# First products of five and six blocks made ahead at the opening of an FFN

## The chip, the cores and the metric

The kernel runs as one program on one core of a Trainium2 chip. The metric is device microseconds of one execution, from the first to the last instruction and what lies around them; a median over several runs stands for a kernel. One further execution was profiled, and its trace is what the rows below are from. Engines are named as the profile names them: PE is the matmul engine and PEld its weight loads, DVE, ACT and POOL are the vector, scalar and GpSimd engines, SP issues the transfers.

## The reference, cut to what matters

Two layers work on 512 latent tokens and, in the first layer, 256 context tokens of width 1024. Each layer mixes tokens with three groups of heads, projects out, and then runs a SwiGLU FFN of hidden width 2816 between two norms. All data are 32-bit floats.

```python
def swiglu(h, w13, w2):
    gate, up = jnp.split(h @ w13, 2, axis=-1)
    return (jax.nn.silu(gate) * up) @ w2

for l in range(DEPTH):
    ...
    lat = lat + gt1 * rms_norm(mixed_l, norm_mix_post[l])
    h_l = modulate(rms_norm(lat, norm_ffn_pre[l]), sh2, sc2)
    lat = lat + gt2 * rms_norm(swiglu(h_l, ffn_w13[l], ffn_w2[l]), norm_ffn_post[l])
    if not last:
        ...
        cx = cx + cgt2 * rms_norm(swiglu(h_c, ffn_w13[l], ffn_w2[l]), norm_ffn_post[l])
```

The change lies in `h @ w13`, the up-projection, where it begins.

## The kernel before

**Precision.** Every operand of a matmul is split into two parts: `hi`, the value cast to a shorter float format (on ACT, L368 for weights, L1303 for activations), and `lo`, the rest (a subtraction on DVE, L369 and L1304). A product is three matmuls per 128 rows of the inner dimension: hi by hi, hi by lo, lo by hi (`prod`, L1320, matmuls at L1324).

**The up-projection.** The hidden width is cut into 22 blocks of 128 (`NF`). For each block, gate and up are made together by Strassen's scheme in Winograd's form: the inner dimension is halved, the tokens are halved (`hn` is 384 in layer 0 and 256 in layer 1), and gate and up are the two halves of the weights. Seven products replace eight. Each is over 4 inner blocks of 128, so it has 12 matmuls. The activations' side gives `b11`, `b21`, `b22` and the sums `t1` to `t4` (`combine`, L1307); the weights' side gives `a11`, `a12` (the gate's two halves), `a22` and the sums `s1` to `s4`, made per block in `load13` (L399): two on POOL (L417, L418) and two on DVE (L419, L420). `s2` to `s4` lie in a tile `S` with one buffer.

**Loads.** `load13` brings a block's weights into a tile `raw`: block numbers that are odd use the one in pool `F`, even ones the one in pool `wp`. Each of the two has one buffer. A full block is two transfers of 512 KB (`fetch(0)` for up, `fetch(2)` for gate, L405). A gate-only load (`gate_only`) is one transfer of 512 KB. The pieces are then cast and subtracted into `whi` and `wlo`, four buffers each, of 1024 columns.

**Made ahead.** The two products with `b11` and `b21` need only the first half of the tokens, whose norms are finished first. For the first `NA` blocks the kernel loads the gate alone (`u["w13a"]`), makes the product `a11` by `b11` (`up_first`, L1327, its result copied to `uu` at L1329) and later adds `a12` by `b21` (`up_gate`, L1331, SiLU into `g1` at L1333). Between the two the result stays open in a bank of the accumulator memory: pool `psm` has two banks (`mm`), `psx` five (`px`), `psa` one (`pa`). When such a block's turn comes in `ffn_up` (L1335) its weights are loaded again, in full, since the sums need all four quarters, but `a11` and `a12` are not split again (`late`), and five products are left. A block with nothing made ahead runs all seven.

**Order.** `begun` is filled in block order (from L1367), then `b21` is split, then the gate products follow, then `combine`, then `ffn_up` for all 22 blocks. The code's order gives priorities; a scheduler at compile time places each instruction on its engine's queue by them and by when it expects operands and buffers to be there. On the chip each queue runs in that fixed order. `get(i, 0)` loads a unit only when it is asked for; `get(i)` also loads the one after it, so full blocks 0 and 1 are asked for together.

**Space.** `uu` and `g1` have `NA + 1` buffers in pool `FB`, on the right side of the memory; `F` holds `raw`, `S`, `hf`, `u3` and `g2`.

Of the kernel before, what the change touches and what calls it, by code (L numbers as in the profile page):

```python
# [11 lines left out]
F32 = mybir.dt.float32  # L12
# [70 lines left out]
def tile_backbone(ctx: ExitStack, tc: tile.TileContext, a: dict, out: bass.AP, dbg=None):  # L83
# [9 lines left out]
    psa = ctx.enter_context(tc.tile_pool(name="psa", bufs=1, space=PSUM))  # L93

    def mm():
        return psm.tile([128, 512], F32, tag="mm", name="mm")

    def px():
        return psx.tile([128, 512], F32, tag="px", name="px")

    def pt(pool, tag, shape, dt=F32, bufs=None):
        kw = {} if bufs is None else {"bufs": bufs}
        return pool.tile(shape, dt, tag=tag, name=tag, **kw)
# [164 lines left out]
    def kblk(src):  # L268
        return src.rearrange("(k p) n -> p k n", p=128)
# [84 lines left out]
    def add(name, shape, srcs, prem=None, hook=None):  # L354
        specs.append((name, shape, srcs, prem, hook))
        return len(specs) - 1
# [75 lines left out]
    def get(i, ahead=1):  # L432
        while state["next"] <= min(i + ahead, len(specs) - 1):
            j = state["next"]
            if specs[j][0] == "wo" and j > i:
                break
            load(j)
            state["next"] += 1
        return state["units"].pop(i)
# [3 lines left out]
    def w_unit(name, src, c0, n, prem=None):  # L443
        return add(name, [128, 8, n], [((allsl,), kblk(src[:, c0:c0 + n]))], prem)
# [3 lines left out]
    for l in range(NL):  # L448
        wi = a["w_in"][l]
        u = U[l]  # L450
        if l > 0:
            u["gv"] = w_unit("gv", wi, 256, 256)
        u["small"] = add("small", [128, 8, 80],
                         [((allsl, allsl, slice(0, 32)), kblk(wi[:, 768:800])),
                          ((allsl, allsl, slice(64, 80)), kblk(wi[:, 2336:2352]))],
                         hook=lambda raw: G.memset(raw[:, :, 32:64], 0.0))
        u["xbc"] = {j: w_unit("xbc", wi, 1312 + 256 * j, 256) for j in (2, 3, 0, 1)}
        u["gqk"] = w_unit("gqk", wi, 0, 256)
        u["rk"] = w_unit("rk", wi, C_RET + 256, 256)
        u["rq"] = w_unit("rq", wi, C_RET, 256)  # L460
        u["rv"] = w_unit("rv", wi, C_RET + 512, 256)
        if l == 0:
            u["gv"] = w_unit("gv", wi, 256, 256)
        u["gr"] = w_unit("gr", wi, 512, 256)
        u["rg"] = w_unit("rg", wi, C_RET + 768, 256)
        for j in range(2):
            u[f"z{j}"] = w_unit("z", wi, 800 + 256 * j, 256)
        u["wo"] = [w_unit("wo", a["w_out"][l], 256 * j, 256, l) for j in range(4)]
        u["w13"], u["w2"] = {}, {}
        w13 = a["ffn_w13"][l]  # L470

        NA = 4
        u["NA"] = NA

        def add13(f, gate_only, late):
            return add("w13", None, {"f": f, "gate_only": gate_only, "late": late,
                                     0: kblk(w13[:, FF + 128 * f:FF + 128 * f + 128]),
                                     2: kblk(w13[:, 128 * f:128 * f + 128])})

        u["w13a"] = [add13(f, True, False) for f in range(NA)]  # L480
        for f in range(NF):
            u["w13"][f] = add13(f, False, f < NA)
        u["passes"] = [(j, range(6 if l + 1 < NL else 4)) for j in range(2)]
        for pi, (j, _) in enumerate(u["passes"]):
            f0 = 0
            for gi, gn in enumerate(GROUPS):
                u["w2"][gi, pi] = add("w2", [128, gn, 512],
                                      [((allsl,), kblk(a["ffn_w2"][l, 128 * f0:128 * (f0 + gn),
                                                                   512 * j:512 * j + 512]))])
                f0 += gn  # L490
# [9 lines left out]
    def gemm_a(unit, csl, m, seg, cut=False):  # L500
        t0, n = seg
        ps = mm()
        w = [(lambda k, t=t: t(k)[:, csl]) for t in unit]
        step = 256 if cut else n
        for o in range(0, n, step):
            h = [(lambda k, t=t: t[:, k, t0 + o:t0 + o + step]) for t in H["t"]]
            gemm3(ps[:m, o:o + step], w, h, 8)
        return ps
# [77 lines left out]
    for l in range(NL):  # L586
# [60 lines left out]
        with ExitStack() as sx:  # L647
# [16 lines left out]
            with pool(f"Sa{l}") as Sa:  # L664
# [14 lines left out]
                for t0, n in segs_all[::-1]:  # L679
                    ps = opened.pop(("small", t0), None) or gemm_a(un, slice(0, 80), 80, (t0, n), True)  # L680
# [7 lines left out]
                for d in range(2):  # L688
                    zz = pt(Sa, f"gz{d}", [128, T])
                    ee = pt(Sa, f"ge{d}", [128, T])  # L690
                    for t0, n in segs_all:
                        ps = px()
# [53 lines left out]
            with scx:  # L746
                for fb in (4, 5, 6, 7, 0, 1, 2, 3):
# [5 lines left out]
                    for t0, n in segs[::-1]:  # L753
# [4 lines left out]
                        ps = gemm_a(un, slice(128 * (fb % 2), 128 * (fb % 2) + 128), 128, (t0, n), fb in (4,))  # L758
# [14 lines left out]
                    if fb < 4:  # L773
                        ps = [px(), px()]
# [99 lines left out]
            for j in range(2):  # L874
                for t0, n in (segs_out if j == 0 else segs_all):
                    ps = gemm_a(un, slice(128 * j, 128 * j + 128), 128, (t0, n))
# [391 lines left out]

        NA = u["NA"]
        hview = hds[l].rearrange("f p t -> p f t")  # L1270
# [14 lines left out]
        with pool(f"F{l}") as F:  # L1285
            state["F"] = F
            def ut(tag, bufs=2):
                return pt(FB if tag in ("uu", "g1") else F, tag, [128, hn], bufs=bufs)

            uus = [ut("uu", NA + 1) for _ in range(NA)]  # L1290
            g1s = [ut("g1", NA + 1) for _ in range(NA)]
            bh = pt(FB, "bh", [128, 2, 4, hn], F32R, bufs=1)
# [27 lines left out]
            def prod(ps, un, wn, rn, first):  # L1320
                w, r = un[wn], rhs[rn]
                for k in range(4):
                    for p, (x, y) in enumerate(((0, 0), (0, 1), (1, 0))):
                        PE.matmul(ps[:, :hn], w[x][:, k], r[y](k), start=first and k == 0 and p == 0,  # L1324
                                  stop=k == 3 and p == 2, skip_group_check=True)

            def up_first(pa, un, uu):  # L1327
                prod(pa, un, "a11", "b11", True)
                S.copy(uu, pa[:, :hn])  # L1329

            def up_gate(pa, un, g1):  # L1331
                prod(pa, un, "a12", "b21", False)
                S.activation(g1, pa[:, :hn], AF.Silu)  # L1333

            def ffn_up(f, begun):  # L1335
                un = get(u["w13"][f])
                hf = pt(F, "hf", [128, tot], bufs=2)
                h1, h2 = hf[:, :hn], hf[:, hn:]
                if begun is None:
                    pa = mm()  # L1340
                    uu, g1 = ut("uu", NA + 1), ut("g1", NA + 1)
                    up_first(pa, un, uu)
                else:
                    uu, g1 = begun
                pb = px()
                prod(pb, un, "s2", "t2", True)
                V.tensor_tensor(uu, uu, pb[:, :hn], ALU.add)
                pc = px()
                prod(pc, un, "s3", "t3", True)
                u3 = ut("u3")  # L1350
                V.tensor_tensor(u3, uu, pc[:, :hn], ALU.add)
                pd = px()
                prod(pd, un, "s1", "t1", True)
                V.tensor_tensor(h2, u3, pd[:, :hn], ALU.add)
                if begun is None:
                    up_gate(pa, un, g1)
                prod(pc, un, "a22", "t4", False)
                V.tensor_tensor(h1, uu, pc[:, :hn], ALU.add)
                G.tensor_tensor(h1, h1, g1, ALU.mult)  # L1359
                prod(pd, un, "s4", "b22", False)  # L1360
                V.tensor_tensor(uu, uu, pd[:, :hn], ALU.add)
                g2 = ut("g2")
                S.activation(g2, uu, AF.Silu)
                G.tensor_tensor(h2, h2, g2, ALU.mult)
                DMA.dma_start(hds[l][f], hf)

            begun = []  # L1367
            for f in range(NA):
                un = get(u["w13a"][f], 0)
                ps = mm() if f < 2 else px()  # L1370
                up_first(ps, un, uus[f])
                begun.append((ps, un))
            for i in range(n2):
# [12 lines left out]
            for f in range(NF):  # L1386
                ffn_up(f, begun.get(f))
                if f == 9:
                    for i in range(2):
                        he = pt(FB, "tm", [128, 2, 2, tot], F32R)  # L1390
                        hr = pt(HR, "hr", [128, 2, tot], bufs=1)
                        hid_load(hr, 2 * i)
                        early[2 * i] = hid_split(hr, he[:, 0], he[:, 1])
# [26 lines left out]
        with pool(f"D{l}") as Dp:  # L1420
# [30 lines left out]
            for pi, (j, poss) in enumerate(u["passes"]):  # L1451
# [3 lines left out]
                f = 0  # L1455
# [45 lines left out]
```

## Time and profile before

| | us |
|---|---|
| runs of the kernel | 1896.44, 1889.72, 1876.48 |
| median | 1889.72 |
| the profiled execution | 1883.05 |
| its span, first to last instruction | 1881.3 |
| PE busy in it | 1744.7 (93%) |
| DVE, ACT, POOL busy | 1169.3, 793.0, 560.7 |
| mean granted PE clock | 0.959 of full speed |

In rows of a timeline the first number is the start in us from the span's start, the second the time until the row's last instruction ends, then engine, line, operation, tile written and tiles read, shapes and a count (x2: two such in a row). What stands in square brackets is how long the engine was idle before the row, and what ended it. The trace writes `u` for `u3`, `g` for `g1` and `g2`, `H` for tiles of that tag whatever their name in the code (`whole`, `ta`, `tb_`), and `cst` and `araw` for the two parts of `b11`.

### The profile page before, as it was taken

Reading aid. Unit: us, or ns where it says so; the run is one execution under the profiler, and the core shown is the slowest. Engines: PE = TensorE matmul, PEld = TensorE weight load, DVE = VectorE, ACT = ScalarE, POOL = GpSimd, SP = SyncE. Lnnn points to the kernel's source line nnn. Section 1 sums busy time; section 2 is a strip of 40 time slices with the busy share of each in tenths; the row PEclk is TensorE's granted clock in tenths of the full one; section 3 lists DMA queues with packets and bytes.
Section 4 is the critical chain, followed back from the end, with each engine's and each line's share of the span. In section 5 each row is a group of like instructions: output and inputs, shape, how many; then the busy total and the mean of one; then the engine's idle time right before and its main releaser. Section 6 shows DMA issues by size and latency. Waiting matters only on the chain. (4 is left out here: it accounts for less than half of the span.)

```text
span 1881.3 us, 30313 instructions
## 1 busy us (share of the span) xinstructions
PE 1744.7 (93%) x11851; PEld 1576.0 (84%) x11851; DVE 1169.3 (62%) x1981; ACT 793.0 (42%) x1433; POOL 560.7 (30%) x569
## 2 busy tenths in 40 slices
PE   4999999999879999999899989999987969999998
PEld 3778887798879999999788777889876969999886
DVE  4586787557557655554334446678766568888455
ACT  3545343225654333333323465444423544444343
POOL 1002622104303432332312240073312226555322
PEclk9999999999989999999999989999977989999999
DMA  8535457415325433332645374345613245444663
GB/s 277 183 103 171 136 188 262 156 46 177 113 68 145 140 105 93 93 93 90 240 140 184 116 235 134 112 147 171 214 53 124 84 129 153 125 138 130 245 209 128
DMA packets 239228, 275.15 MB, mean 146 GB/s; under 512 B 14056, under 2 KB 182476, under 8 KB 239084
## 3 DMA queue, kind: packets, MB, share of 16 engines
q1 hardware_dynamic: 237872, 271.30, 45.0%
q8 instruction: 93, 1.52, 0.3%
q10 hardware_dynamic: 1212, 1.91, 0.3%
q14 instruction: 51, 0.42, 0.1%
HBM read 234.24 MB, written 38.93 MB: 145 GB/s over the span
## 5 line engine op out<-in xcount | busy, mean ns | idle before, releaser
L369 DVE TENSOR_TENSOR wlo<-raw,whi 128x1024 fp32r<-128x1024 f32 (+2 forms) x192 | 264.1, 1382 | 160.0 <-ACT whi L368 159.7
L1324 PE MATMUL px<-H,whi 128*128 128x384 f32 (+1 forms) x1408 | 307.6, 310 | 7.4 <-ACT whi L368 7.3
L368 ACT CAST whi<-raw 128x1024 fp32r<-128x1024 f32 (+2 forms) x192 | 194.0, 1018 | 221.6 <-PE px L1324 86.3
L498 PE MATMUL mm<-whi,H 128*128 128x256 f32 x1376 | 275.5, 295 | 11.3 <-ACT stg L630 5.3
L498 PEld LDWEIGHTS mm<-whi,H 128*128 128x128 f32 x1376 | 224.1, 197 | 26.1 <-issue 12.7
L1324 PEld LDWEIGHTS px<-H,whi 128*128 128x128 f32 x1408 | 235.1, 190 | 10.2 <-ACT whi L368 9.5
L1324 PE MATMUL px<-H,wlo 128*128 128x384 f32 (+1 forms) x704 | 211.5, 310 | 0.9 <-DVE wlo L369 0.8
L498 PE MATMUL mm<-wlo,H 128*128 128x256 f32 x688 | 200.6, 292 | 0.0
L498 PE MATMUL mm<-H,whi 128*128 128x256 f32 (+2 forms) x640 | 160.9, 342 | 6.8 <-ACT xp L759 4.4
L368 ACT CAST whi<-S 128x1024 fp32r<-128x1024 f32 x88 | 73.5, 835 | 165.3 <-DVE S L419 84.6
L498 PEld LDWEIGHTS mm<-wlo,H 128*128 128x128 f32 x688 | 135.4, 197 | 3.1 <-issue 2.1
L1324 PEld LDWEIGHTS px<-H,wlo 128*128 128x128 f32 x704 | 131.6, 190 | 1.7 <-DVE wlo L369 1.7
L498 PEld LDWEIGHTS mm<-H,whi 128*128 128x128 f32 (+1 forms) x640 | 109.5, 190 | 26.0 <-ACT xp L759 6.2
L1278 POOL TENSOR_TENSOR hidlo<-hr,hidhi 128x768 fp32r<-128x768 f32 (+1 forms) x40 | 69.7, 1745 | 191.1 <-ACT hidhi L1277 184.7
L498 PE MATMUL px<-whi,H 128*128 128x256 f32 x640 | 120.5, 288 | 3.9 <-ACT H L1235 2.2
L1359 POOL TENSOR_TENSOR hf<-hf,g 128x384 f32<-128x384 f32 (+1 forms) x44 | 55.2, 1255 | 223.2 <-issue 147.0
L369 DVE TENSOR_TENSOR wlo<-S,whi 128x1024 fp32r<-128x1024 f32 x88 | 89.3, 1015 | 40.6 <-ACT whi L368 40.5
L1407 PE MATMUL px<-wlo,hidhi 128*128 128x512 f32 x276 | 108.7, 394 | 0.0
L498 PE MATMUL mm<-H,wlo 128*128 128x256 f32 (+3 forms) x320 | 108.3, 339 | 0.0
L1407 PE MATMUL px<-whi,hidhi 128*128 128x512 f32 x276 | 107.8, 393 | 0.0
L498 PEld LDWEIGHTS px<-whi,H 128*128 128x128 f32 x640 | 101.3, 193 | 6.3 <-ACT H L1235 3.2
L1407 PE MATMUL px<-whi,hidlo 128*128 128x512 f32 x276 | 106.1, 389 | 0.0
(334 smaller groups left out, 4086.0 us busy)
## 6 DMA issues: line engine op xcount, KB each, us to landing
raw<-ffn_w_dram SPq DMA_DIRECT2D x100, 512.0 KB
araw<-ada_w_dram SPq DMA_DIRECT2D x96, 512.0 KB
raw<-w_in_dram SPq DMA_DIRECT2D x26, 1024.0 KB
raw<-ffn_w_dram SPq DMA_DIRECT2D x20, 1024.0 KB
hr<-hd SPq DMA_DIRECT2D x22, 768.0 KB
hr<-hd SPq DMA_DIRECT2D x22, 512.0 KB
Rt<-gd SPq DMA_DIRECT2D x40, 256.0 KB
hd<-hf SPq DMA_DIRECT2D x22, 384.0 KB
```

The source lines that it names most:

```text
L368: S.copy(hi, src)
L369: lo_engine.tensor_tensor(lo, src, hi.bitcast(F32), ALU.subtract)
L498: PE.matmul(ps, x(k), y(k), start=(k == 0 and p == 0), stop=(k == total - 1 and p == 2))
L1278: (G if q else V).tensor_tensor(lo[:, q], hr[:, q], hi[:, q].bitcast(F32), ALU.subtract)
L1324: PE.matmul(ps[:, :hn], w[x][:, k], r[y](k), start=first and k == 0 and p == 0, stop=k == 3 and p == 2, skip_group_check=True)
L1359: G.tensor_tensor(h1, h1, g1, ALU.mult)
L1407: PE.matmul(ps, lh[x](k), rh[y](k), start=f + k == 0 and p == 0, stop=f + k == NF - 1 and p == 2, skip_group_check=True)
```

## The change

The number of blocks made ahead is 5 in layer 0 and 6 in layer 1, in place of 4 in both. `u3` has one buffer in place of two. Block 2's product is kept open in the `pa` bank in place of a `px` bank; blocks 0 and 1 stay in `mm`, and blocks from 3 on are in `px`.

```diff
-        NA = 4
+        NA = 5 if l == 0 else 6
         u["NA"] = NA
...
                 prod(pc, un, "s3", "t3", True)
-                u3 = ut("u3")
+                u3 = ut("u3", 1)
                 V.tensor_tensor(u3, uu, pc[:, :hn], ALU.add)
...
             for f in range(NA):
                 un = get(u["w13a"][f], 0)
-                ps = mm() if f < 2 else px()
+                ps = mm() if f < 2 else px() if f > 2 else psa.tile([128, 512], F32, tag="pa", name="pa")
                 up_first(ps, un, uus[f])
                 begun.append((ps, un))
```

`NA` also sets which full blocks are `late`, the number of gate-only units, and the buffers of `uu` and `g1`. There is one gate-only transfer of 512 KB more in layer 0 and two in layer 1.

## Rows read from the trace of the kernel before

**Rows 1.** The page: busy time and share of the span by engine.

```profile
PE 1744.7 (93%) x11851; PEld 1576.0 (84%) x11851; DVE 1169.3 (62%) x1981; ACT 793.0 (42%) x1433; POOL 560.7 (30%) x569
```

**Rows 2.** Busy time by stretch: both openings, and layer 0's steady part between them.

```profile
core 0: us, PE busy (x) PEld busy (x) DVE busy (x) ACT busy (x) POOL busy (x), PEclk, DMA share, GB/s
543.30:576.55 33.25, 19.55 (x96) 17.80 (x94) 25.13 (x43) 21.52 (x38) 3.65 (x4) 0.79 0.39 111
660.00:700.00 40.00, 40.00 (x232) 40.00 (x231) 24.70 (x32) 15.09 (x21) 10.17 (x10) 1.00 0.25 74
1501.10:1533.43 32.33, 18.19 (x115) 16.07 (x113) 22.40 (x37) 18.71 (x35) 5.24 (x4) 0.79 0.40 114
```

**Rows 3.** PE's waits, layer 0's opening: us in total, times, longest.

```profile
PE px L306 <- ACT xn L297: 4.9, 1, 4.9
PE px L1324 <- ACT whi L368: 3.2, 1, 3.2
```

**Rows 4.** PE's waits, layer 1's opening.

```profile
PE px L1324 <- ACT whi L368: 2.5, 2, 2.3
```

**Rows 5.** POOL's timeline: the first sum of a full block, both layers.

```profile
572.06 1.29 POOL L417 TENSOR_TENSOR S<-raw 128x512 f32<-128x512 f32 x1 [22.74 <-DMA raw<-ffn_w_dram]
...
602.50 1.29 POOL L417 TENSOR_TENSOR S<-raw 128x512 f32<-128x512 f32 x1
...
612.90 1.30 POOL L417 TENSOR_TENSOR S<-raw 128x512 f32<-128x512 f32 x1
...
671.70 1.29 POOL L417 TENSOR_TENSOR S<-raw 128x512 f32<-128x512 f32 x1
...
861.48 1.29 POOL L417 TENSOR_TENSOR S<-raw 128x512 f32<-128x512 f32 x1
...
1528.93 1.28 POOL L417 TENSOR_TENSOR S<-raw 128x512 f32<-128x512 f32 x1 [17.30 <-DMA raw<-ffn_w_dram]
...
1554.94 1.29 POOL L417 TENSOR_TENSOR S<-raw 128x512 f32<-128x512 f32 x1 [0.63 <-DVE wlo L369]
...
1563.23 2.27 POOL L417 TENSOR_TENSOR S<-raw 128x512 f32<-128x512 f32 x1
...
1616.06 1.29 POOL L417 TENSOR_TENSOR S<-raw 128x512 f32<-128x512 f32 x1
...
1735.10 1.29 POOL L417 TENSOR_TENSOR S<-raw 128x512 f32<-128x512 f32 x1
```

**Rows 6.** SP's timeline: requests for weights, layer 0 (block 2, 3, full 0, full 1).

```profile
535.27 0.38 SPq L405 DMA_DIRECT2D raw<-ffn_w_dram  x1
...
563.20 0.38 SPq L405 DMA_DIRECT2D raw<-ffn_w_dram  x1
...
564.34 0.99 SPq L405 DMA_DIRECT2D raw<-ffn_w_dram  x2
...
569.68 0.99 SPq L405 DMA_DIRECT2D raw<-ffn_w_dram  x2
```

**Rows 7.** SP's waits, layer 0's opening: us in total, times, longest.

```profile
SPq L405 <- DVE wlo L369: 14.1, 3, 11.0
```

**Rows 8.** SP's timeline: requests for weights, layer 1 (block 3, full 0, full 1).

```profile
1520.42 0.38 SPq L405 DMA_DIRECT2D raw<-ffn_w_dram  x1
...
1521.56 1.01 SPq L405 DMA_DIRECT2D raw<-ffn_w_dram  x2
...
1527.13 0.99 SPq L405 DMA_DIRECT2D raw<-ffn_w_dram  x2
```

**Rows 9.** ACT's timeline: casts of gate-only weights and block 0's SiLU.

```profile
556.69 1.99 ACT L368 CAST whi<-raw 128x1024 fp32r<-128x1024 f32 x2
...
561.95 0.49 ACT L1333 ACTIVATE g<-mm 128x384 f32<-128x384 f32 x1 [0.57 <-PE mm L1324]
...
567.29 1.05 ACT L368 CAST whi<-raw 128x1024 fp32r<-128x1024 f32 x1 [1.55 <-DMA raw<-ffn_w_dram]
...
1524.79 1.05 ACT L368 CAST whi<-raw 128x1024 fp32r<-128x1024 f32 x1 [1.43 <-DMA raw<-ffn_w_dram]
```

**Rows 10.** DVE's timeline, layer 1: the subtraction of block 3's gate weights.

```profile
1525.87 1.22 DVE L369 TENSOR_TENSOR wlo<-raw,whi 128x1024 fp32r<-128x1024 f32 x1 [0.87 <-ACT whi L368]
```

## The prediction

> **What bounds the kernel now.** I read the page first. TensorE (PE) is busy for 1744.7 us of the 1881.3 us span [rows 1], so the kernel is bound by matmuls and can gain only where PE waits, about 137 us spread over the whole span. Next came the table of stretches, for the places that the change touches. In the stretch that opens layer 0's FFN PE works 19.55 us of 33.25, in layer 1's 18.19 of 32.33, both at a mean granted clock of 0.79; in the middle of layer 0's up-projection it works 40.00 of 40.00 [rows 2]. So the two openings hold some 28 us of idle PE, and the rest of the up-projection none worth naming in layer 0. The change can pay only in these two openings.
>
> The third view is who PE waited for there. The longest wait is for the last token block's normalised rows (4.9 us in layer 0) and the last one before the first full block is for a `whi` cast: 3.2 us in layer 0 [rows 3], 2.5 us in layer 1 [rows 4]. That last wait ends the opening, so I followed it backwards. The cast needs the sums made on POOL, and POOL's first L417 starts at 572.06 only when its data lands, after 22.74 us of idleness [rows 5]. The data was asked for at 564.34 [rows 6], and that request stood waiting on SyncE's queue (SP) for a `wlo` subtraction on VectorE (DVE): 14.1 us in three waits [rows 7]. The `wlo` frees the landing tile `raw`. There are two `raw` tiles, one for even blocks and one for odd, each with a single buffer. **The opening is bound by the turns of these two tiles**, not by a lack of products that PE could make: load, cast on ScalarE (ACT), subtract on DVE, next load. Layer 1 shows the same: requests at 1520.42, 1521.56 and 1527.13 [rows 8], POOL starting at 1528.93 after 17.30 us idle, on the DMA [rows 5].
>
> **The change, part by part.**
>
> *A fifth gate-only load in layer 0, a fifth and a sixth in layer 1.* Block 4's gate load goes through the even tile after block 2's and ahead of full block 0; block 5's goes through the odd tile ahead of full block 1. So full block 0's request moves back by one turn of the even tile. The landing is priced with the gate load of block 3: requested at 563.20 [rows 6], its cast started at 567.29, ended by the DMA [rows 9], so 4.09 us; in layer 1 1520.42 to 1524.79, 4.37 us [rows 8, 9]. The new load is requested 1.14 us behind that one and shares the queue: 4.09 + 1.14 = 5.2 us. Add the cast of 1.05 us [rows 9] and the subtraction of 1.22 us [rows 10]: 5.2 + 1.05 + 1.22 = 7.5 us for a turn. The floor, with no sharing, is 4.09 + 1.05 + 1.22 = 6.4. The ceiling takes the landing of full block 0, twice the bytes: 572.06 - 564.34 = 7.72 [rows 5, 6], so 10.0. I take 7.5, the row of the same size. It delays the first full block by 7.5 us in each layer; what follows on POOL, DVE and ACT is as long as before. In layer 1 the odd tile's turn for block 5 runs beside it, since full block 1 is wanted some 8 us later than full block 0.
>
> The Trainium skill, "DMA: Bandwidth & Descriptors", section Anatomy of one DMA, fits a DMA by a fixed 2.0 us and its bytes over 436e9 a second, measured on another issue path than SP's. By that estimate 512 KB land in 3.2 us where this trace has 4.09 and 4.37 with traffic beside them, a turn is 5.5 us, and the total below would be +3.5 instead of +7.5; the trace is nearer to the case, so its row is used.
>
> *Products moved ahead.* Every product is 12 matmuls. A full block with nothing made ahead has seven products, one begun ahead has five left. PE's work is the same in total; it moves. I read what a block costs from the rhythm of POOL's L417, once per block [rows 5]. Layer 0: blocks with nothing ahead follow each other by (861.48 - 671.70) / 13 = 14.60 us; blocks begun ahead by 612.90 - 602.50 = 10.40. So turning block 4 from one kind to the other saves 4.20 us, exactly the two products of 14.60 / 7 = 2.09 each that moved. Layer 1: (1735.10 - 1616.06) / 12 = 9.92 against 1563.23 - 1554.94 = 8.29. Two products are worth 2 x 9.92 / 7 = 2.83 there, but only 1.63 us is saved: five products take 7.09, and the block still follows the last by 8.29, because the loop over the single `S` tile (POOL's sums, DVE's sums, casts, subtractions, POOL again) is then the longer one; POOL's L417 waits for that `wlo` [rows 5]. Two blocks save 3.26 us.
>
> The moved products themselves fall into the wait before the first full block: they are ready at about the end of the turn, 4.2 us (layer 0) or 5.7 us (layer 1) of PE work, and PE is then held back longer than that by the later load. Their price is 0 while this cover stands. If they ended after block 0's data were ready, they would delay it by at most 4.2 and 5.7 us.
>
> *The rest at nothing.* The fifth and sixth pairs of `whi` and `wlo` buffers come from blocks 0 and 1, whose gate products must be done: block 0's are at 561.95, when ACT takes its result [rows 9], before the new load lands. Block 2's sums move from a `px` bank to `pa`, which no one uses in this stretch; `u3` with one buffer is written and read by DVE alone, in order. More `uu` and `g1` buffers cost space, not time. The 1.5 MB more of loads stand beside DMA engines that are busy 0.25 to 0.40 of these stretches [rows 2]. Bounds for these together: 0 to 1 us, by one `whi` cast standing in ACT's order ahead of its data (ACT waited 1.55 us for block 3's load [rows 9]); below nothing only if the scheduler happens to order better, which is a rival below. I take 0.
>
> *Sum.* Layer 0: +7.5 - 4.20 = +3.3. Layer 1: +7.5 - 3.26 = +4.2. Together +7.5 us; by the turn's bounds 6.4 and 10.0 it is +5.3 and +12.5. The profiled execution took 1883.05 us, its span 1881.3 with 1.75 around it, and would take 1890.6. It lies 6.7 us below the median of the three runs, 1889.72, and the forecast is made against that median: **1897.2 us**, its own range 1895 to 1902.
>
> **The rivals.**
>
> *Earlier turns: faster.* Block 2's gate load was asked for at 535.27 [rows 6] and by 4.09 us landed at about 539.4, but its cast stands at 556.69 beside block 1's [rows 9], 17 us later. If the new order of instructions puts that cast when its data is there, the even tile's turns all come earlier, the added turn delays nothing, and the savings stay: -4.2 - 3.26 = -7.5, so 1882.3. For it: ACT's work in that opening does not fill it (21.52 of 33.25 us [rows 2]). Against it: nothing in the change touches block 2's load or cast; what held the cast back before holds it after. It decides from the point at which block 2's cast moves by more than a turn, 7.5 us.
>
> *Full block 1 asked for first: slower still.* In layer 0 the odd tile is free at 569.68, when full block 1 was requested [rows 6]; full block 0 would now be requested at 564.34 + 7.5 = 571.8. If SP's order is turned to follow this, 1 MB for block 1 is in front of block 0's 1 MB. The price is up to one landing of 7.72 us in layer 0; in layer 1, where block 5's load holds the odd tile past 1529, none is expected, but with the same order there it would be as much. Then the sum is +7.5 + 7.7 = +15.2 or, in both layers, +22.9: 1905 to 1912.6. For it: the two requests would become ready in the other order. Against it: the products of block 1 could then go first, which takes most of the price back. It is slower than before by over 1% (18.9 us) only where both layers pay in full.
>
> *The turn is hidden anyway: no change.* If the openings' end is set by something that I took for slack, for instance the products of the right-hand sides, or if the landings share the queue less than thought, turn and savings cancel and the time is 1889.7. For it: the savings are 7.5 us and the products moved 9.9, half and two thirds of the two delays' 15. Against it: POOL's wait ended with the DMA in both layers [rows 5].
>
> That the change doesn't do what it says would need the scheduler to place blocks 4 and 5 after full block 0; they are issued ahead of it in the code, and their `raw` turn is ahead in either case, so I give it no chance of its own.
>
> **How the numbers follow.** Chances: the forecast 0.55, earlier turns 0.15, full block 1 first 0.15, no change 0.15. Single runs of before spread from 1876.48 to 1896.44, so a median of a few runs can stand some 5 us off. The range goes to the rival below, 1882.3 less 3, and on the other side to 1909, between the two prices of the slower rival: 1879 to 1909. About 1% of the time, 18.9 us, is what a measurement of this kernel can tell from no change. Faster by that much would need more than twice all that the faster rival gives: 0.02. Slower by it is the second form of the slower rival and chance: 0.05. Within 1%: 0.93.
>
> **What would show it.** Right: in layer 0 a request for block 4's half load at about 564.3 and full block 0's near 571.8; POOL's first L417 at about 579.5 in layer 0, and 7.5 us later in layer 1 against its opening; a longer wait of PE for a `whi` cast before the first full block; five blocks at 10.4 us in layer 0 and six at about 8.3 in layer 1. Wrong: a first L417 that stands less than 4.2 us (layer 0) or 3.3 us (layer 1) later, which would make the change a gain; block 2's cast before 550; or blocks 4 and 5 of layer 1 following each other by some 7.1 us, which would mean that the `S` loop has no hold on them.

## The result, and the profile after

The changed kernel takes 1894.8 us (median of 20 runs, 1886.14 to 1904.12), the kernel before, run beside it, 1884.31 (20 runs, 1876.48 to 1896.44). The ratio is 1.0053 with a 95% interval of 1.0036 to 1.0071, so the change costs 10 us, between 6.8 and 13.4. The forecast was +7.5 us. The sum and the sign came out; the terms did not all, and a stage that the forecast never named, layer 1's down-projection, takes 4.7 of the 8.3 us that the profiles below show.

The profiled execution of after took 1886.75 us, near the low end of its runs. Executions also differ ahead of the change: the first up-projection matmul of layer 0 started between 535.1 and 549.7 us in the fourteen profiles of this study, though nothing before it was changed. So spans of single profiles are no measure here, and each stage below rests on one profile of each kernel. I cut each profile into stages at the starts of the first and last up-projection and down-projection matmuls (the first and last starts that the view of a source line gives) and compared stages. "First sum" is the time from the first up-projection matmul to POOL's first L417.

| us | first sum, layer 0 | up, layer 0 | down, layer 0 | first sum, layer 1 | up, layer 1 | down, layer 1 |
|---|---|---|---|---|---|---|
| before | 28.8 | 344.3 | 189.0 | 27.0 | 250.5 | 119.4 |
| after | 35.6 | 344.7 | 188.7 | 33.1 | 254.0 | 124.1 |
| forecast of the difference | +7.5 | +3.3 | 0 | +7.5 | +4.2 | 0 |
| measured | +6.8 | +0.4 | -0.3 | +6.1 | +3.5 | +4.7 |

The four stages together are 8.3 us longer, which agrees with the +10 of the medians.

**The openings.** On the page, PE is as busy as before, as it must be [rows 1]:

```profile
PE 1743.2 (92%) x11851; PEld 1573.3 (83%) x11851; DVE 1162.2 (62%) x1981; ACT 791.8 (42%) x1433; POOL 563.6 (30%) x569
```

POOL's timeline of after, the first two sums of layer 0 and the first of layer 1, to be held against [rows 5]:

```profile
576.59 1.29 POOL L417 TENSOR_TENSOR S<-raw 128x512 f32<-128x512 f32 x1 [29.60 <-DMA raw<-ffn_w_dram]
584.10 1.27 POOL L417 TENSOR_TENSOR S<-raw 128x512 f32<-128x512 f32 x1 [4.88 <-DVE wlo L369]
...
1530.72 1.29 POOL L417 TENSOR_TENSOR S<-raw 128x512 f32<-128x512 f32 x1 [23.39 <-DMA raw<-ffn_w_dram]
```

POOL is idle 29.60 us for the data instead of 22.74, and 23.39 instead of 17.30. SP's timeline says why; here is layer 0 (blocks 3 and 4, full 1, full 0), against [rows 6]:

```profile
560.55 1.50 SPq L405 DMA_DIRECT2D raw<-ffn_w_dram  x2
...
567.09 0.99 SPq L405 DMA_DIRECT2D raw<-ffn_w_dram  x2
...
570.11 1.00 SPq L405 DMA_DIRECT2D raw<-ffn_w_dram  x2
```

and layer 1 (block 5, full 0, full 1), against [rows 8]:

```profile
1522.43 0.37 SPq L405 DMA_DIRECT2D raw<-ffn_w_dram  x1
...
1524.78 0.99 SPq L405 DMA_DIRECT2D raw<-ffn_w_dram  x2
...
1528.61 0.99 SPq L405 DMA_DIRECT2D raw<-ffn_w_dram  x2
```

Counted from the first up-projection matmul (541.0 in after, 543.3 before), full block 0 is asked for at +29.1 instead of +21.0. Its request leaves when DVE's subtraction for block 4 has freed the even tile. DVE's timeline of after:

```profile
568.86 1.23 DVE L369 TENSOR_TENSOR wlo<-raw,whi 128x1024 fp32r<-128x1024 f32 x1 [1.79 <-ACT whi L368]
```

That ends at 570.09 and the request stands at 570.11. The turn is confirmed step by step. It also shows the slower rival's order in layer 0: full block 1 went out first, at 567.09, when the odd tile came free (block 3's subtraction ends at 567.06). No run isolates the price of that order; it is far below the 7.72 us that the rival put on it, for full block 0's data took 576.59 - 570.11 = 6.48 us, less than the 7.72 of before.

**The down-projection of layer 1.** PE's waits from the last up-projection matmul to the last down-projection matmul, before (us in total, times, longest):

```profile
PE pa L1407 <- ACT whi L368: 1.2, 1, 1.2
```

The same view of after:

```profile
PE pa L1407 <- ACT hidhi L1277: 4.8, 2, 3.2
```

Its windows at the longer of the two waits (the columns of [rows 2]):

```profile
1760.00:1762.00 2.00, 0.13 (x1) 0.00 (x0) 0.17 (x1) 1.25 (x2) 0.00 (x0) 1.00 1.06 408
1762.00:1764.00 2.00, 0.65 (x2) 0.57 (x3) 2.00 (x2) 1.82 (x3) 0.10 (x1) 0.94 1.06 408
1764.00:1766.00 2.00, 2.00 (x6) 1.56 (x5) 2.00 (x3) 1.14 (x2) 2.00 (x2) 0.50 1.03 412
1766.00:1768.00 2.00, 2.00 (x7) 1.56 (x7) 1.56 (x1) 0.00 (x0) 2.00 (x2) 0.71 1.02 408
1768.00:1770.00 2.00, 2.00 (x10) 1.66 (x9) 0.00 (x0) 0.00 (x0) 1.81 (x1) 1.00 1.03 389
```

PE waits 3.2 us for the split of the hidden rows and then runs at a granted clock of 0.50, which is the level of 1.2 GHz, with 6 matmuls in 2 us, where 10 stand in the last row, at 1.00.

### The profile page after: what moved, and what is told of

Read it like the earlier page. It is cut to its first block, busy times and chain, and to the rows that moved or that the text cites. A ratio compares the mean times of both kernels' runs of the same rounds, so it can differ in the third digit from the quotient of the medians.

```text
span 1884.9 us, 30326 instructions
## 1 busy us (share of the span) xinstructions
PE 1743.2 (92%) x11851; PEld 1573.3 (83%) x11851; DVE 1162.2 (62%) x1981; ACT 791.8 (42%) x1433; POOL 563.6 (30%) x569
## 6 DMA issues: line engine op xcount, KB each, us to landing
raw<-ffn_w_dram SPq DMA_DIRECT2D x103, 512.0 KB
araw<-ada_w_dram SPq DMA_DIRECT2D x96, 512.0 KB
hr<-hd SPq DMA_DIRECT2D x22, 512.0 KB
```

## The experiments

Each ratio is to the kernel before on the same chip. Line numbers shift by a few lines where code was added. The edits are cut to the lines that matter; `...` marks what is left out.

**1. Layer 0 alone.**

```diff
-        NA = 5 if l == 0 else 6
+        NA = 5 if l == 0 else 4
```

> Five blocks ahead in layer 0, four in layer 1, the two side edits (one u3 buffer, block 2 in the pa bank) kept. Theory (turn of the even landing tile): layer 0's first L417 stands about 7 us later after the first up-projection matmul than before (before 572.06 - 543.3 = 28.8, so 35 to 36), the saved block gives 4.2 back, and layer 0's up-projection takes 344.3 us (before) plus 0 to 3.5; layer 1's up- and down-projection as before (250.5 and 119.4). Ratio 1.000 to 1.002. Rival (the cost is in layer 0, or in the order of all that follows): 1.004 or more with this half alone.

Measured: 1886.31 us, ratio 1.0011 (0.9989 to 1.0033). The first sum came at 35.8, but layer 0's up-projection took 343.7, and layer 1 was as before (251.0, 119.1). The fifth block in layer 0 is neither gain nor loss.

**2. Layer 1 alone.**

```diff
-        NA = 5 if l == 0 else 6
+        NA = 4 if l == 0 else 6
```

> Four blocks ahead in layer 0, six in layer 1, side edits kept. Theory: layer 0 as before; layer 1's up-projection 3 to 4.5 us longer than 250.5; if the later weights' request that stands ahead of the last hidden loads on SP's queue comes from layer 1's six blocks, its down-projection too takes 4 to 5 us more than 119.4. Ratio 1.003 to 1.005. Rival (the longer down-projection is not this change's but comes and goes between executions, or comes from layer 0): down-projection 118 to 120, ratio 1.001 to 1.002.

Measured: 1894.79 us, ratio 1.0062 (1.0037 to 1.0088). Up-projection 256.9 (+6.4), down-projection 124.4 (+5.0). All that the change costs is in layer 1.

**3. The extra turns without the products.** The kernel before, with block 4's (and 5's) gate loaded, cast and subtracted in the opening and then not used; the blocks run their seven products as before.

```diff
+        u["w13x"] = [add13(f, True, False) for f in range(NA, 5 if l == 0 else 6)]
...
+            for i in u["w13x"]:
+                get(i, 0)
```

> The kernel before with its four blocks ahead, and only the added gate-only loads put in (one in layer 0, two in layer 1), cast and subtracted but not used; no product moves. Theory: the first L417 moves as in the changed kernel, by 6 to 7.5 us in each layer, nothing is given back: up-projections longer by 5 to 7.5 us each, ratio 1.005 to 1.008. Rival (the loads are hidden and the cost comes from the products' places or the banks): both up-projections within 2 us of before, ratio 0.999 to 1.002.

Measured: 1896.24 us, ratio 1.0063 (1.0037 to 1.0088). The first sums came at 35.7 and 34.2, and the up-projections grew by 6.5 and 7.1; the down-projection of layer 1 did not (119.1). So the turn by itself costs near what the forecast put on it (7.5), and the cost in the down-projection does not come from the turn.

**4. The turn taken away.** Blocks 4 and 5 land in a tile of their own, a buffer (`hr`) that stands empty until the tenth block. It is one buffer: in layer 1 both blocks take their turn in it.

```diff
+        if srcs["gate_only"] and f >= 4:
+            raw = pt(state["HR"], "hr", [128, 2, 512], bufs=1)
+            DMA.dma_start(raw.rearrange("p s (k n) -> p (s k) n", n=128), srcs[2])
+            t0 = split(wp, raw, [128, 2, 512], V)
+            return {n: tuple(t0[q][:, o].rearrange("p (k n) -> p k n", n=128) for q in range(2))
+                    for n, o in (("a11", 0), ("a12", 1))}
...
+            state["HR"] = HR
```

> The changed kernel, but the gate-only loads of blocks 4 and 5 land in the tile that holds hidden rows later (one buffer, idle in the opening), so that full block 0's request follows block 2's as before. Theory: layer 0's first L417 at 28 to 31 us after the first up-projection matmul (before 28.8, changed 35.6), layer 1's likewise near before's 27.0 (1528.93 - 1501.9); up-projections shorter than before's 344.3 and 250.5 by 2 to 4 us each; ratio against before 0.995 to 0.999, or 0.998 to 1.001 if layer 1's down-projection keeps its 4.7 us. Rival (the turn is not what costs): as the changed kernel, 1.004 to 1.006.

Measured: 1886.07 us, ratio 1.0005 (0.9983 to 1.0027). The delay of the first sum is gone: 28.6 and 26.8. Layer 0 then gains 4.6 us (339.7), close to the forecast's saving of 4.20. Layer 1 gains nothing (251.4), and its down-projection still takes 124.1. POOL's timeline of this kernel shows where layer 1's saving went:

```profile
1529.38 1.28 POOL L423 TENSOR_TENSOR S<-raw 128x512 f32<-128x512 f32 x1 [17.08 <-DMA raw<-ffn_w_dram]
1540.34 1.29 POOL L423 TENSOR_TENSOR S<-raw 128x512 f32<-128x512 f32 x1 [8.31 <-DVE wlo L369]
```

The second sum follows the first by 10.96 us, where it took 7.52 before: 3.4 us, as much as the two blocks save. ACT's timeline of this kernel says what held it:

```profile
1535.09 1.04 ACT L368 CAST whi<-hr 128x1024 fp32r<-128x1024 f32 x1 [1.70 <-DMA hr<-ffn_w_dram]
1536.04 1.04 ACT L368 CAST whi<-S 128x1024 fp32r<-128x1024 f32 x1
```

The same cast of `S` before:

```profile
1532.33 1.05 ACT L368 CAST whi<-S 128x1024 fp32r<-128x1024 f32 x1 [2.90 <-DVE S L419]
```

It stands 6.66 us after the first sum instead of 3.40. In front of it on ACT is the cast of block 5's gate, whose load could be asked for only at 1528.53, when block 4's subtraction (it ends at 1528.50) had freed the one own tile. So in layer 1 a turn was still in the way, moved to another tile. Behind the second sum the saving is there: from the second sum to the last, layer 1 takes 195.7 us instead of 198.7.

**5. Five blocks in layer 1, four in layer 0.**

```diff
+        NA = 4 if l == 0 else 5
```

> Four blocks ahead in layer 0, five in layer 1, side edits kept. On SP's queue the request for the third piece of the down-projection's weights stands behind the last hidden store and the next two hidden loads again, as before. Theory: layer 1's first L417 about 7 us later (34 us after the first matmul, before 27.0), one block gives 1.6 back, up-projection 3 to 6 us longer than 250.5; down-projection 119 to 120, since only the order of that queue made it 124. Ratio 1.002 to 1.004. Rival (the longer down-projection comes from the space or the delay that more blocks bring): down-projection above 122.

Measured: 1889.53 us, ratio 1.0022 (1.0001 to 1.0043). The one profile shows an up-projection of 259.4, longer than expected and not explained, and a down-projection of 121.4. There PE waits 1.5 us, as with four blocks; the rest is more busy time for the same work, at a mean granted clock of 0.99 where the runs with four blocks have 1.00.

**6. The order of requests in the down-projection.** In after, SP asks for the third w2 unit ahead of the last hidden rows' store and loads, which it did not before. Here that request was put behind two of those loads, and the unit before it no longer asks for it ahead of time.

```diff
-            un = get(u["w2"][1, 0])
+            un = get(u["w2"][1, 0], 0 if last else 1)
...
+                        with tc.issue_after(state["hid", 6].ins):
+                            un = get(u["w2"][gi, pi])
...
```

> The changed kernel with one thing set by hand: in layer 1 the request for the third piece of the down-projection's weights is issued behind the next two hidden loads, the place that it had before. Theory: down-projection back to 119 to 121 us (before 119.4, changed 124.1), PE's wait for the hidden casts (4.8 us) gone; the rest as in the changed kernel, so ratio 1.002 to 1.004 where the changed kernel has 1.0053. Rival (the request's place is not what costs): down-projection still 123 to 125, ratio 1.005.

Measured: 1893.99 us, ratio 1.0036 (1.0011 to 1.0062); down-projection 124.0. PE's wait only moved: `hidhi` 4.7 us in two waits, since four other loads now stood ahead of the next hidden rows.

**7. A version of the gain alone:** five blocks in layer 0, four in layer 1, block 4 in its own tile (the edit of 4).

```diff
+        NA = 5 if l == 0 else 4
```

> Five blocks ahead in layer 0, the fifth's gate load in the tile that holds hidden rows later; four in layer 1. Theory: layer 0's up-projection 339 to 341 us as in the run with both layers (344.3 before), layer 1 as before. Ratio 0.996 to 0.999, faster than both kernels. Rival (the order of all that follows shifts and eats it): layer 1's stages 3 us or more above before's, ratio 1.000 to 1.002.

Measured: 1877.55 us, ratio 0.9971 (0.9953 to 0.9989). Layer 0's up-projection takes 339.7; the rest is as before. It is faster than both kernels.

**8. Block 2 in the own tile too**, in both layers, so that the even tile is free earlier. Against 7:

```diff
-        if srcs["gate_only"] and f >= 4:
+        if srcs["gate_only"] and f in (2, 4, 5):
```

> As the run with layer 0's fifth block in its own tile, and block 2's gate load goes there too, in both layers, so that full block 0's request needs to wait only for block 0's gate split. Theory (the turns of the even tile bound the opening): the first L417 comes earlier than before in both layers, under 26 us after the first matmul in layer 0 and under 25 in layer 1, and each up-projection is 2 to 4 us shorter than without this edit; ratio 0.994 to 0.997. Rival (by then the casts' and subtractions' own queues, or the four whi buffers, bind): no gain over the run with the fifth block alone.

Measured: 1876.9 us, ratio 0.9958 (0.9940 to 0.9975), the fastest of the study, though its interval overlaps that of 7. The first sums come at 6.0 and 9.6 us, some 20 us earlier, yet layer 0's up-projection stays at 339.9, and layer 1's takes 248.3. POOL's timeline in layer 0 shows that the wait has moved:

```profile
546.47 1.26 POOL L423 TENSOR_TENSOR S<-raw 128x512 f32<-128x512 f32 x1
...
579.41 1.29 POOL L423 TENSOR_TENSOR S<-raw 128x512 f32<-128x512 f32 x1 [30.33 <-DVE wlo L369]
```

The second sum waits 30.33 us for the subtraction that frees `S`. Before that subtraction come the casts of `S`, and ACT's timeline has block 4's cast ahead of the first of them, behind a second turn of the own tile, which block 2 had first:

```profile
568.26 1.05 ACT L368 CAST whi<-hr 128x1024 fp32r<-128x1024 f32 x1 [2.21 <-DMA hr<-ffn_w_dram]
...
569.73 1.05 ACT L368 CAST whi<-S 128x1024 fp32r<-128x1024 f32 x1
```

So the `raw` tiles no longer hold the first sum, but the own tile's turn stands in front of the casts; how much of the wait it makes was not tried.

**9. The whole order of requests restored** in layer 1's down-projection, with five and six blocks: as 6, and the token loads put behind the hidden rows.

```diff
...
+                        with tc.issue_after(state["hid", 8 if i < 2 else 10].ins):
+                            xs.append(x_tile(nf, xsd[128 * tb:128 * tb + 128, :], 4))
```

> The changed kernel; in layer 1's down-projection the whole order of requests on SP's queue is set back to that of before (third piece of weights behind two hidden loads, the four x loads behind the next two). The run before this one moved only the first of these, and the wait of PE for hidden casts went on one step later (4.7 us in all). Theory (what stands ahead of the hidden loads costs the 4.7 us): down-projection 119 to 120.5 us, no wait of PE for hidden casts above 1.5 us; ratio 1.001 to 1.004. Rival (the order is a sign and not the cause): 123 to 125 again, ratio 1.004 to 1.006.

Measured: 1891.89 us, ratio 1.0062 (1.0037 to 1.0087); down-projection 123.6. SP's order was that of before, and the cost stayed. PE's wait for the hidden rows did fall, from 4.8 to 1.0 us, but a wait of 2.3 us for `whi` (1.2 before) and one of 0.8 for `hidlo` stand there now. My theory that the order of requests alone makes the cost is refuted.

**10. The side edits alone** (`u3` with one buffer, block 2 in the `pa` bank, four blocks).

```diff
-        NA = 5 if l == 0 else 6
+        NA = 4
```

> Four blocks ahead in both layers, as before, with only the side edits: one u3 buffer, block 2 in the pa bank. Priced at nothing by the theory: both up-projections within 1 us of 344.3 and 250.5, down-projection within 1 us of 119.4, ratio 0.998 to 1.002. Rival (a bank or the single u3 buffer makes someone wait): ratio 1.003 or more.

Measured: 1882.14 us, ratio 1.0010 (0.9994 to 1.0027); every stage within 0.5 us of before. They cost nothing.

**11. Everything at once:** five and six blocks, blocks 2, 4 and 5 in the own tile, the order of 9. Against the edit of 4:

```diff
-        if srcs["gate_only"] and f >= 4:
+        if srcs["gate_only"] and f in (2, 4, 5):
...
```

> The changed kernel's five and six blocks, with the gate loads of blocks 2, 4 and 5 in the tile of the hidden rows, and layer 1's order on SP's queue set as in the run just above. Theory (layer 1's sixth and fifth blocks pay once the even tile's turn and the order are out of the way): layer 1's up-projection 246 to 249 us, below the 248.3 of the run with four blocks there, ratio 0.994 to 0.996. Rival (in layer 1 blocks begun ahead follow each other by the S loop, so more of them give next to nothing): up-projection 248 to 251, ratio 0.996 to 0.998.

Measured: 1883.52 us, ratio 1.0016 (0.9998 to 1.0034). Layer 0 is at 339.2, layer 1 at 252.5 and 121.5. Layer 1 again gains nothing over before (250.5), and loses 4.2 us against 8 with four blocks (248.3). But three loads now share the one own tile, and as in 4 the first cast of `S` (1533.89) stands on ACT right behind block 5's, which waited 1.57 us for its data. From the second sum to the last, layer 1 takes 196.3 us against 199.6 in 8. What six blocks would give with a tile for each was not tried.

**12. One pair of instructions turned round on DVE.** With six blocks, DVE does a w2 subtraction ahead of the last sum of the last block (L1361), which the last store of hidden rows needs. DVE's timeline before:

```profile
1752.70 0.42 DVE L1361 TENSOR_TENSOR uu<-uu,px 128x256 f32<-128x256 f32 x1 [3.02 <-PE px L1324]
1755.37 2.36 DVE L369 TENSOR_TENSOR wlo<-raw,whi 128x1024 fp32r<-128x1024 f32 x2 [2.25 <-ACT whi L368]
```

The same of after:

```profile
1752.45 1.23 DVE L369 TENSOR_TENSOR wlo<-raw,whi 128x1024 fp32r<-128x1024 f32 x1 [1.49 <-ACT whi L368]
1753.59 0.42 DVE L1361 TENSOR_TENSOR uu<-uu,px 128x256 f32<-128x256 f32 x1
```

And in the kernel of this run:

```profile
1753.30 0.42 DVE L1361 TENSOR_TENSOR uu<-uu,px 128x256 f32<-128x256 f32 x1 [0.97 <-PE px L1324]
1753.83 2.36 DVE L369 TENSOR_TENSOR wlo<-raw,whi 128x1024 fp32r<-128x1024 f32 x2
```

```diff
...
-            un = get(u["w2"][0, 0])
+            with (tc.issue_after(state["tail"].ins) if last else ExitStack()):
+                un = get(u["w2"][0, 0])
```

Here `state["tail"]` is the last block's L1361; the rest is as in 9.

> As the kernel with five and six blocks and the down-projection's order of requests restored, with one pair of instructions on DVE turned round at the end of layer 1's up-projection: the last block's last sum (L1361) ahead of the subtraction of the down-projection's second weights, in place of behind it. Theory (late last row): with six blocks the last store of hidden rows leaves 4.2 us after the last up-projection matmul starts, before it was 2.0, because that sum waits on DVE; the loads of those rows, their casts and the products follow later by as much. Then the store comes 2.5 to 3.0 us after that matmul, PE's waits from there to the end of the down-projection fall from 4.1 us to 2.0-3.0 and the stretch from the last up-projection matmul to the last down-projection matmul from 123.6 us to 121.5-122.5; the time falls by 1 to 2 us against 1.006 of before. Rival (the last sum is no part of it, the cost lies in which products PE has left): the store comes earlier, the stretch stays at 123-124.5.

Measured: 1892.22 us, ratio 1.0051 (1.0020 to 1.0081); down-projection 120.7, against 123.6 in 9 and 119.4 before. PE's waits there, this kernel:

```profile
PE pa L1407 <- ACT whi L368: 2.4, 1, 2.4
PE pa L1407 <- ACT hidhi L1277: 0.3, 1, 0.3
```

The waits fell from 4.1 to 2.7 us, as expected, and the stage by 2.9, more than expected. The step between was not as expected: the store came 3.8 us after the last up-projection matmul (1756.81 against 1753.0), not 2.5 to 3.0, because ACT's SiLU of the same block (L1363, at 1754.64) stood behind the casts of the same w2 unit. The other 1.5 of the 2.9 us are PE's busy time for the same work, 118.0 instead of 119.5, and that is the clock. After a wait of 2.35 us for `whi` the kernel of 9 ran at 0.62 and 0.53 for 4 us, while this one, after 2.38 us, stayed at 1.00. Windows of 9:

```profile
1786.00:1788.00 2.00, 1.51 (x4) 1.22 (x5) 1.53 (x2) 2.00 (x4) 0.00 (x0) 0.62 0.08 29
1788.00:1790.00 2.00, 2.00 (x7) 1.57 (x5) 2.00 (x2) 1.47 (x3) 1.44 (x2) 0.53 0.02 8
```

A window of 12:

```profile
1780.00:1784.00 4.00, 3.09 (x12) 2.27 (x13) 3.18 (x3) 3.83 (x6) 1.08 (x1) 1.00 0.13 50
```

A window of 11, after a wait of 2.29 us:

```profile
1781.00:1785.00 4.00, 3.82 (x15) 2.85 (x16) 3.90 (x3) 3.10 (x6) 1.82 (x2) 1.00 0.27 26
```

Run 11 shows how little of this need be the pair's. It has SP's order of 9 and DVE's pair as in after, and it too stayed at 1.00: its stage took 121.5 us, with 3.5 us of waits and 118.0 busy. Against it the pair brings 0.8 us, all of it waits, by one profile of each. Over all runs the stage took 119.1 to 120.5 us in the six profiles with four blocks in layer 1 (before, 1, 3, 7, 8 and 10) and 121.5 to 124.4 in the six with six blocks and the pair not turned (after, 2, 4, 6, 9 and 11). The times of 9 and 12 are not told apart by their intervals.

## Why the prediction was right, and where it was not

**The sum: near, and in part by luck.** Added to a median of three runs, 1889.72, the forecast gave 1897.2; twenty runs put the kernel before at 1884.31. A base 5.4 us too high and a difference some 3 too low met near the measured 1894.8. Within the difference the stages missed by -2.9 (layer 0), -0.7 (layer 1) and +4.7 (its down-projection), which nearly cancel.

**The bound: right.** The turns of the two landing tiles held the openings. Taking the tile away (4, 7) removes the delay of the first sum; adding only the load (3) makes it. The next bound lies close behind: in 8 the first sum of layer 0 comes 22.5 us earlier than in 7, and the stage is no shorter. One reading was off: the last wait of layer 1's opening is 2.3 us; 2.5 is the sum of two [rows 4].

**The turn: right in place, a little large.** Forecast 7.5 us, measured 6.8 and 6.1. Its two parts miss in opposite ways. From block 4's request to full block 0's it took 8.4 us in layer 0 (561.67, the second request of the first row of SP's timeline, to 570.11); in layer 1 the request moved by 7.5, from 1521.56 - 1501.9 = 19.7 to 1524.78 - 1497.6 = 27.2 after the first matmul. But the full block then landed faster, in 6.48 us instead of 7.72 and in 1530.72 - 1524.78 = 5.94 instead of 7.37, and the forecast had left that landing as it was. What stands ahead of it on the queue had changed: in layer 0 full block 1's megabyte, asked for 3.0 us earlier, in place of a half load asked for 1.1 us earlier. That this made the difference is argued, not shown. What the runs show is that the load in front counts: in the seven openings with full block 1 ahead (after, 1, 3, 6, 9 and 12 in layer 0, 5 in layer 1) the first sum starts 9.4 to 9.7 us after full block 1's request, though full block 0's own request follows that one by anything from 2.0 to 3.0 us. The Trainium skill's fit ("DMA: Bandwidth & Descriptors", Anatomy of one DMA) made the total +3.5 as an estimate; the measured interval of 6.8 to 13.4 does not hold it.

**Layer 0, +0.4 instead of +3.3: the step that failed is "what follows on POOL, DVE and ACT is as long as before", where PE's own order was left out.** The saving is there: without the turn, in 4 and 7, the stage is 4.6 us shorter, of which 3.6 and 3.2 are waits and the rest is less busy time for the same work. In after a second product came back. PE's timeline before, from the end of its wait:

```profile
576.55 1.76 PE L1324 MATMUL px<-H,whi 128*128 128x384 f32 x6 [3.24 <-ACT whi L368]
578.15 0.36 PE L1324 MATMUL px<-bh,whi 128*128 128x384 f32 x1
...
581.51 0.45 PE L1324 MATMUL px<-bh,wlo 128*128 128x384 f32 x1
581.79 0.34 PE L1324 MATMUL px<-H,wlo 128*128 128x384 f32 x1
```

The matmuls with `bh` are a gate product by `b21`. One such product, 12 matmuls, stood on PE's queue behind block 0's first six, and so behind the wait. In after, both remaining ones lie ahead of it:

```profile
574.05 0.44 PE L1324 MATMUL px<-bh,whi 128*128 128x384 f32 x1 [1.05 <-ACT uu L1329]
...
578.17 0.33 PE L1324 MATMUL px<-bh,wlo 128*128 128x384 f32 x1
581.08 1.57 PE L1324 MATMUL px<-H,whi 128*128 128x384 f32 x6 [2.58 <-ACT whi L368]
```

Block 0 starts 40.1 us after the first matmul instead of 33.25, which is +6.85. Off go the 4.20 of block 4 and one product of 2.09: +0.6, and +0.4 was measured. The longer wait was filled with one product more than I counted. Run 3, which moves that product too but not block 4's, agrees only with a further term: 6.85 - 2.09 is 4.8, and it lost 6.5. PE waited 4.83 us there, its first six matmuls of block 0 took 2.29 us instead of 1.76, and over the two stages of layer 0 it was busy for 513.6 us instead of 512.0 with the same work, 1.6 more, at a mean granted clock of 0.97 instead of 0.98. PE's idle time in layer 0's up-projection bears the account out: 15.6 us before and 15.6 in after, 20.3 in run 3, which is the 4.8.

**Layer 1, +3.5 instead of +4.2: right, roughly.** 6.1 of delay less 3.26 of saving is +2.8. The saving is there in this profile: from the first sum to the last, layer 1 takes 202.9 us instead of 206.2, though the blocks begun ahead follow each other by 7.6 to 10.0 and not evenly by 8.3. The other 0.7 is work that changed stage: three matmuls more of the down-projection, 0.23 us each, run before the last up-projection matmul. Other executions of the same six blocks had +6.4 (2), +5.2 (6), +5.7 (9) and +3.6 (12), with 204.5, 204.4, 204.9 and 203.2 us from the first sum to the last, so the saving there was 1.3 to 3.0. What makes up these differences was not settled. One term at nothing was mis-sized for runs 4 and 11: the forecast bounded a `whi` cast standing in ACT's order ahead of its data at 1 us, and in 4 such a cast held `S` by 3.3 us.

**The down-projection of layer 1, +4.7 instead of 0: not seen at all.** It comes with six blocks, whether or not the first sum is late (4), and not with the extra loads (3) or the side edits (10). Of the 4.7 us, 3.6 are waits of PE and 1.1 are more busy time, though three matmuls fewer fall into the stage. PE waits 0.8 to 1.9 us there in the six profiles with four blocks in layer 1, 3.8 to 4.8 in four with six (after, 2, 4 and 6), 4.1 and 3.5 with SP's order restored (9 and 11) and 2.7 with the pair on DVE turned round as well (12). Its busy time is 118.0 to 118.6 us where the mean granted clock was 1.00 (the six with four blocks, 11 and 12) and 119.3 to 120.6 where it was 0.97 to 0.99 (after, 2, 4, 5, 6 and 9). So the two orders take part in the waits, each by one or two profiles, and neither is the whole cause. What stays open: the wait of 2.3 us for `whi` that is left in 12 (1.2 before), why the clock falls in some of these executions, and why the scheduler places the w2 work ahead of the last block's results when six blocks are made ahead. A cast held back on ACT in the same manner was not tried.

**The rivals.** Earlier turns did not happen. Full block 1 asked for first did, in layer 0, at a price that no run isolates. "The turn is hidden" is nearly what layer 0 came to, though by another way: the turn was paid in full and filled with work.

## What to carry to other kernels

Before making work ahead of a wait, ask what the data for it has to pass through: a load into a single landing buffer puts itself in front of the load that ends the wait, and here an empty buffer elsewhere took the loss of 0.5% away (4); leaving layer 1 at four blocks as well made it a gain of 0.3 to 0.4% (7, 8). Check that the new place has room for every load sent there: with one load in the own tile layer 0 gained 4.6 us, with two layer 1 gained nothing, because the second waited for the first and its cast stood on ACT in front of the sums. And after a change far upstream, compare every stage down to the end, since a compile-time scheduler may turn round pairs hundreds of microseconds later, and look at the clock of a stage in several runs before an edit is credited with it.

## What the hardware and the schedule showed beside it

Waits on PE cost more than their length when the clock falls with them: 3.2 us of waiting in after was followed by 4 us at 0.50 and 0.71. Three waits of nearly the same length, 2.35, 2.38 and 2.29 us, were followed by 0.62 and 0.53 in run 9 and by 1.00 in runs 12 and 11, so the length of the wait alone did not decide it here.

In seven openings a load of one megabyte was asked for 2.0 to 3.0 us behind another. Its consumer started 9.4 to 9.7 us after the request in front, whatever the distance, which was 6.5 to 7.5 us after its own.
